# A hybrid HGRN2, mLSTM and expert-choice MoE layer: the mixer loop put in another order, router logits with tokens on partitions, g1 folded into w_out, head norms applied at the store

## The chip, the cores and the metric

The program runs on one core of a Trainium2 chip. The metric is device time in microseconds (us) of one execution, taken as the median of several runs. Beside the times there is one profiled execution, whose trace gives every instruction of the engines: PE (TensorE matmuls; PEld is its weight load), DVE (VectorE), ACT (ScalarE), POOL (GpSimd), and SP, whose queue issues nearly all DMAs here.

## The reference

One layer for 1024 latent tokens of width 1024 and 256 context tokens, all in float32:

```python
u = rms_norm(x, norm1_w) * (1 + sc1) + sh1            # adaLN, sh1..g2 from c @ ada_w + ada_b
p = u @ w_in                                          # HGRN2 q,i,g,f(2 directions); mLSTM q,k (3x3 conv), v, o, gates
hg = hgrn2 forward + hgrn2 backward                   # 4 heads of 128
ml = mlstm forward + mlstm backward                   # 4 heads of 128
hg = hg * rsqrt(mean(hg*hg, head) + eps) * hg_norm_w * silu(p_g)
ml = layer_norm(ml, head) * ml_norm_w * sigmoid(p_o)
x  = x + g1 * (concat(hg, ml) @ w_out)
v  = rms_norm(x, norm2_w) * (1 + sc2) + sh2
aff = softmax(v @ router_w)                           # 16 experts
gate, idx = top_k(aff.T, 128)                         # each expert takes its 128 best tokens
y  = (silu(v[idx] @ w_gate) * (v[idx] @ w_up)) @ w_down * gate
x  = x + g2 * scatter_add(y, idx)
out = rms_norm(x, final_norm_w)
```

## The kernel before, in words

The code states the work in one order; a planner then lays every engine's instructions out as a fixed list. It runs a simulated clock over the program and gives an engine, at each moment, the first instruction in program order that it thinks ready. On the chip each list is then executed strictly in order, whatever the real times are. DMAs issued by SP are such a list too. Tiles are named; a name with `bufs=n` has n slots, and a new tile waits until the oldest one is read for the last time.

Matmuls that must be exact to float32 split each operand in a high and a low part (`wh`/`wl`, `mh`/`ml`) and add three products.

The stages, with their lines:

- Modulation, context work and projections (to 180 us), then the HGRN2 heads, four in turn (lines 649 to 701, to 455 us). At the end of a head, for each half of the tokens, ACT squares the output `po` with a running sum into `hgr` (698), copies it to `ob` (700, one slot named `hgo`), and SP stores it in DRAM as `d_hg` (701). After all heads, DVE and POOL turn `hgr` into 1/rms at once (720, 721).
- The convolution stage (lines 798 to 1099, to about 713 us). `ORD` (1077) is an order written by hand: a number n is `conv(n)` (812) for one group of 128 mLSTM channels; "v..." and "o..." are pieces of the V projection and the output gates (863); "kN" transposes and scales the keys of token block N (`back_k`, 840) and "uN" makes the backward state before that block from them (`back_u`, 845); "M" opens the pools of the mixer and loads the first three row blocks of w_out (`load_wo`, 1073); "S0", "S1" are `scores`, "O0" is `outputs`, "L0" `normed`.
- The mixer loop (1135 to 1179), over eight blocks of 128 tokens. `scores(cc)` (932) loads `qkx` and `MB`, the latter the row maxima broadcast over 128 partitions; makes q.k on PE (939); the decay `E` on ACT and DVE (943 to 945, 949); and `MB` through POOL, ACT and DVE (946, 947, 950). `outputs(cc)` (954) updates the forward state (`ml_u`, 964) and makes the heads (975, 976 on PE, 977 to 981 on ACT and DVE). `normed` (986) layer-norms them (POOL power at 155, ACT 995). `mixed(cc)` (998) multiplies by the gates on DVE (1005 for the HGRN2 heads with `hgr`, 1006 for the mLSTM heads), transposes on PE (1011) and splits into `mh`, `ml` (1012 ACT, 1013 DVE; one slot each). `mixer(cc)` (1016) is the product with w_out (1026: 2 x 24 matmuls), times g1 (1027), plus x (1028), stored as `d_acc` (1029). `router` (1047) norms the row and stores `d_v` (1052 to 1056). `logits` (1032) transposes the row (1038, 1039), multiplies it with the router weights to 16 x 128 (1042) and copies that to SBUF (`lt`, 1044); `affinity` (1062) transposes it back to 128 x 16 on PE (1063) and takes the softmax (1065 to 1069).
- Ahead of the loop w_out's eight row blocks are scaled by the head norm weights and split into `woh`, `wol` (1117 ACT, 1118 DVE) through three slots `wor`.
- In iterations 5 and 6 the loop also sorts affinities for the top-k and makes the first four split expert weights. After it come the rest of the top-k (to 942 us) and the 16 experts (to 1500 us), with 512 KB weight loads running ahead through a list of free buffers (`raw_load`, 883), and the final norm.

The loop's program order in iteration cc is: `scores(cc+2)`, `outputs(cc+1)`, `mixer(cc)`, `router` and `logits` of cc-1, `normed` and `mixed` of cc+1, `affinity(cc-1)`.

## Time and profile before

| | us |
|---|---|
| median of 3 runs | 1559.41 (1558.56 to 1561.38) |
| the profiled execution | 1559.33 |
| its span, first to last instruction | 1557.6 |

| engine | busy, us | share of the span |
|---|---|---|
| PE matmul | 1447.8 | 93% |
| PEld weight load | 1206.9 | 77% |
| DVE | 1230.4 | 79% |
| ACT | 864.7 | 56% |
| POOL | 174.8 | 11% |

Matmuls overlap in the pipeline, so a busy PE row does not mean that PE runs at its peak; and PE's clock has two levels, 1.2 and 2.4 GHz, so a stretch is read by its busy time and by its granted clock together. An average over the program says little here: the stages have different limits, and the change touches the stretch from about 260 to 950 us. Times in the rows are us from the span's start. In a timeline row, what stands in brackets is how long the engine was idle just before it and whose end released it.

### The profile page before, as it was taken

How to read it: one execution, taken by the hardware profiler on the slowest of the kernel's cores; microseconds unless marked ns; L12 is line 12 of the kernel's file. 1: busy time of each engine (PE TensorE's matmuls, PEld its weight loads, DVE VectorE, ACT ScalarE, POOL GpSimd, SP SyncE). 2: the span in 40 equal slices, each digit the busy share in tenths (PEclk: the TensorE clock that was granted, in tenths of full speed). 3: DMA queues.
4: the chain of work that ended last, by engine and by line, in shares of the span. 5: the costliest groups of instructions: out<-in, count | busy, mean ns of one | idle time of the engine just before them, and what ended most of it. 6: DMA issues, size and time to landing. Idle time of an engine off the chain costs nothing.

```text
span 1557.6 us, 23134 instructions
## 1 busy us (share of the span) xinstructions
PE 1447.8 (93%) x8121; PEld 1206.9 (77%) x8121; DVE 1230.4 (79%) x2193; ACT 864.7 (56%) x1454; POOL 174.8 (11%) x136
## 2 busy tenths in 40 slices
PE   7999999999999998988888947999999999999996
PEld 2899878888898896977677735888888888888764
DVE  3685577888866859546757796999999999998887
ACT  3764424334434343345545315777787787777775
POOL 0000000000002221210222110010000000000003
PEclk9999999999999998989898977999999999999998
DMA  9741311220334254276753486999999999999942
GB/s 268 258 128 31 110 54 35 75 82 22 115 102 142 82 149 149 72 194 211 223 183 112 158 320 211 370 391 374 386 387 384 385 389 383 387 376 362 352 141 109
DMA packets 181201, 337.31 MB, mean 217 GB/s; under 512 B 13560, under 2 KB 108348, under 8 KB 181084
## 3 DMA queue, kind: packets, MB, share of 16 engines
q1 hardware_dynamic: 176472, 319.99, 58.0%
q0 software_dynamic: 4320, 15.73, 4.1%
q8 instruction: 64, 1.05, 0.3%
q14 instruction: 53, 0.43, 0.1%
q10 hardware_dynamic: 292, 0.10, 0.0%
HBM read 303.38 MB, written 32.39 MB: 216 GB/s over the span
## 4 chain that ended last, share of the span: by engine, by line
PE 64%; DVE 13%; DMA 10%; issue 6%; ACT 4%; POOL 2%; SPq 0%; ACTq 0%; POOLq 0%; DVEq 0%
PE mm L1303 22%; PE mm L278 11%; PE hg L1303 10%; PE mm L286 5%; PE hg L350 3%; DMA MB<-d_nm 3%; DVE cacc L827 3%; PE hg L215 2%; PE ms L1288 2%; DMA wraw<-in_w_in_dram 1%; PE mm L1026 1%; PE ms L382 1%; POOL cacc L825 1%; DMA wraw<-in_ada_w_dram 1%; PE mm L496 1%
## 5 line engine op out<-in xcount | busy, mean ns | idle before, releaser
L286 PE MATMUL mm<-whi,uh 128*128 128x256 f32 (+1 forms) x512 | 145.6, 284 | 3.0 <-DVE Sb L386 1.3
L286 PE MATMUL mm<-wlo,uh 128*128 128x256 f32 (+1 forms) x512 | 145.1, 283 | 0.0
L286 PE MATMUL mm<-whi,ul 128*128 128x256 f32 (+1 forms) x512 | 144.8, 283 | 0.0
L253 DVE TENSOR_TENSOR wlo<-wraw,whi 128x512 fp32r<-128x512 f32 x96 | 64.7, 686 | 49.5 <-ACT whi L252 49.0
L286 PEld LDWEIGHTS mm<-whi,uh 128*128 128x128 f32 x512 | 96.7, 189 | 5.2 <-DVE Sb L386 1.5
L286 PEld LDWEIGHTS mm<-whi,ul 128*128 128x128 f32 x512 | 96.8, 189 | 0.0
L286 PEld LDWEIGHTS mm<-wlo,uh 128*128 128x128 f32 x512 | 96.3, 188 | 0.3
L1303 PE MATMUL mm<-qkx,xT 128*128 128x512 f32 x256 | 83.7, 408 | 0.6 <-ACT xT L1289 0.3
L827 DVE SCALAR_TENSOR_TENSOR cacc<-pad,cols,cacc 128x1024 f32<-128x1024 f32 x48 | 63.6, 1325 | 24.4 <-POOL cacc L825 23.6
L1303 PE MATMUL mm<-E,xT 128*128 128x512 f32 x256 | 81.2, 398 | 0.4 <-ACT E L922 0.4
L1303 PE MATMUL mm<-MB,xT 128*128 128x512 f32 x256 | 80.8, 397 | 0.0
L252 ACT CAST whi<-wraw 128x512 fp32r<-128x512 f32 x96 | 58.4, 620 | 38.3 <-PE mm L278 24.8
L344 ACT COPY hgc<-hgK 128x512 f32<-128x512 f32 x56 | 35.5, 634 | 78.1 <-DVE hgK L363 38.6
L350 PE MATMUL hg<-hgQ,hgc 128*128 128x128 f32 x448 | 65.9, 291 | 1.0 <-DVE hgQ L366 1.0
L350 PEld LDWEIGHTS hg<-hgQ,hgc 128*128 128x128 f32 x448 | 57.8, 191 | 10.8 <-issue 6.9
L278 PE MATMUL mm<-uh,whi 128*128 128x512 f32 x192 | 63.4, 405 | 0.0
L278 PE MATMUL mm<-ul,whi 128*128 128x512 f32 x192 | 63.4, 404 | 0.0
L278 PE MATMUL mm<-uh,wlo 128*128 128x512 f32 x192 | 61.5, 399 | 0.0
L297 DVE SCALAR_TENSOR_TENSOR ac<-wraw,csil,ac 128x256 f32<-128x256 f32 x112 | 55.9, 499 | 4.1 <-DMA wraw<-in_ada_w_dram 2.2
L1303 PEld LDWEIGHTS mm<-E,xT 128*128 128x128 f32 x256 | 47.9, 189 | 13.7 <-ACT E L922 1.7
L1303 PEld LDWEIGHTS mm<-MB,xT 128*128 128x128 f32 x256 | 48.2, 188 | 11.9
L359 DVE COPY_PREDICATED hgA<-lm,hg 128x512 f32<-128x512 uint8 x56 | 41.4, 740 | 18.4 <-PE hg L350 17.1
(602 smaller groups left out, 4304.2 us busy)
## 6 DMA issues: line engine op xcount, KB each, us to landing
wraw<-in_w_in_dram SPq DMA_DIRECT2D x48, 512.0 KB
wl<-in_exp_w_up_dram SPq DMA_DIRECT2D x34, 512.0 KB
wh<-in_exp_w_up_dram SPq DMA_DIRECT2D x34, 512.0 KB
wh<-in_exp_w_gate_dram SPq DMA_DIRECT2D x34, 512.0 KB
wl<-in_exp_w_gate_dram SPq DMA_DIRECT2D x34, 512.0 KB
wraw<-in_ada_w_dram SPq DMA_DIRECT2D x32, 512.0 KB
wl<-in_exp_w_down_dram SPq DMA_DIRECT2D x29, 512.0 KB
wh<-in_exp_w_down_dram SPq DMA_DIRECT2D x29, 512.0 KB
```

Of the source, the lines that this page charges most:

```text
L215: T.matmul(pm[0:2, :256], csil[:, k, :], adas[i, k // 4][:, k % 4, :, :], start=(k == 0), stop=(k == 7))
L252: S.copy(hi[:, :, cs], src)
L253: V.tensor_sub(lo[:, :, cs], src, hi[:, :, cs])
L278: T.matmul(o, l, r[:, k, i * n:(i + 1) * n], start=(k == 0 and q == 0), stop=(k == 7 and q == 2))
L286: T.matmul(o, l[:, k, ts], r, start=(k == 0 and q == 0), stop=(k == 7 and q == 2))
L297: V.scalar_tensor_tensor(ac, a2[:, k % 4, :], csil[:, k, 0:1], ac, op0=OP.mult, op1=OP.add)
L344: S.copy(view(kc, 0, [[h, 2], [2 * h, 256 // h], [1, h]]), view(K, 0, [[512 + h, 2], [2 * h, 256 // h], [1, h]]))
L350: T.matmul(pb[:, cc, :], kc[:, cc * P:(cc + 1) * P], view(Q, cc * P, pat), start=True, stop=True)
L359: V.copy_predicated(A, lmask[h].unsqueeze(1).to_broadcast([P, 4, P]), scores(h))
L827: V.scalar_tensor_tensor(acc, tap(t), tapw(t, r), acc, op0=OP.mult, op1=OP.add)
L1288: T.transpose(pt[:, k, :], view(src, 4 * q + k, [[8, P]]), ident)
L1303: T.matmul(o, l[:, k, :], r[:, 512 * j:512 * j + 512], start=(k == 0 and p_ == 0), stop=(k == 7 and p_ == 2))
```

## The change

What it does, in the order of the code:

- At the end of a half head, 1/rms is made at once (DVE add of eps, POOL power on 128 x 4) and POOL multiplies `ob` by it ahead of the store. The two instructions after the last head go.
- `mixed` multiplies the HGRN2 heads by their gates in one 128 x 512 instruction, on DVE for cc up to 2 and on POOL from 3, in place of four with `hgr`.
- `mh`, `ml` have two pairs; the second takes two of the three `wor` slots.
- g1 is multiplied into each row block of w_out on POOL (128 x 1024) right after its load; the product with g1 after the mixer's matmuls goes. g1's broadcast is loaded at "M", ahead of the w_out loads.
- `logits` makes 128 x 16 directly (the transposed row as the stationary operand); the copy to `lt` and the transpose in `affinity` go.
- `ORD`: each state update "u" comes a step later after its "k", behind a convolution or another piece; "S1" stands ahead of "O0".
- The loop: `scores(2)` and `normed(outputs(1))` are put ahead of it, and iteration cc is `mixer(cc)`, `scores(cc+3)`, `mixed(cc+1)`, `normed(outputs(cc+2))`, then `router`, `logits`, `affinity` of cc-1.
- One expert weight is loaded in iteration 0 and not three; two `wor` slots and g1's join the free buffers after the loop.

The diff, cut to its core:

```diff
@@ heads' store
                 S.copy(ob, po)
+                r = hgr[:, 4 * hf:4 * hf + 4, h:h + 1]
+                V.tensor_scalar(r, r, EPS, None, op0=OP.add)
+                G.tensor_tensor(r, r, mhalf[:, 0:4].unsqueeze(2), op=OP.pow)
+                G.tensor_mul(ob, ob, r.to_broadcast([P, 4, P]))
                 load(d_hg[4 * hf:4 * hf + 4, :, h * P:(h + 1) * P].rearrange("c p v -> p c v"), ob)
...
-    V.tensor_scalar(hgr, hgr, EPS, None, op0=OP.add)
-    G.tensor_tensor(hgr, hgr, mhalf[:, 0:1].unsqueeze(2).to_broadcast([P, 8, 4]), op=OP.pow)
@@ mixed
-        for h in range(4):
-            V.scalar_tensor_tensor(mix[:, h, :], hg[:, h, :], hgr[:, cc, h:h + 1], go[:, h, :], op0=OP.mult, op1=OP.mult)
+        (G if cc > 2 else V).tensor_mul(mix[:, 0:4, :], hg, go[:, 0:4, :])
...
-        mh, ml_ = tb("mh", [8, P], 1, F32R), tb("ml", [8, P], 1, F32R)
+        mh, ml_ = mixT[cc % 2]
@@ mixer
-            V.tensor_mul(pb, pb, g1b[:, cs])
             V.tensor_add(xm[:, cs], xm[:, cs], pb)
@@ logits
-            T.matmul(pl[0:16, 0:P], rwa[:, k, :], xT[:, k, :], start=(k == 0), stop=(k == 7))
-        lt = tb("lt", [P], 2)
-        S.copy(lt[0:16, :], pl[0:16, 0:P])
-        return pl, lt
+            T.matmul(pl[:, 0:16], xT[:, k, :], rwa[:, k, :], start=(k == 0), stop=(k == 7))
+        return pl
@@ affinity
-        T.transpose(pl[:, P:P + 16], lt[0:16, :], ident[:16, :16])
...
-        V.scalar_tensor_tensor(lg, pl[:, P:P + 16], r2, cb, op0=OP.mult, op1=OP.add)
+        V.scalar_tensor_tensor(lg, pl[:, 0:16], r2, cb, op0=OP.mult, op1=OP.add)
@@ load_wo
         load(wors[k], w_out[k * P:(k + 1) * P, :])
-
-    ORD = (5, 4, "v004", 6, "v044", 7, "v104", 0, "v144", "k7", 1, "u7", "k6", "k5", "u6", "k4", 2, "u5", 3,
-           "o004", "u4", "k3", "o044", "u3", "k2", "u2", "o104", "k1", "M", "u1", "S0", "O0", "L0", "S1", "o144")
+        G.tensor_mul(wors[k], wors[k], g1b)
+
+    ORD = (5, 4, "v004", 6, "v044", 7, "v104", 0, "v144", 1, "k7", "k6", 2, "u7", "k5", "u6", 3, "k4", "u5",
+           "o004", "k3", "u4", "o044", "k2", "u3", "k1", "u2", "o104", "M", "u1", "S0", "S1", "O0", "L0", "o144")
@@ ahead of the loop
+    mixT = [(tb("mh", [8, P], 1, F32R), tb("ml", [8, P], 1, F32R))]
+    mx = {0: mixed(0, sc.pop(0))}
...
+    mixT.append([tl("wor", [1024], 3, F32R).rearrange("p (a b) -> p a b", b=P) for _ in range(2)])
+    free.append([tl("wor", [1024], 3)])
...
+    sc[2] = scores(2)
+    hs = {1: normed(outputs(1, *sc.pop(1)))}
     for cc in range(8):
+        prev_xm, xm = xm, mixer(cc, *mx.pop(cc))
+        if cc < 5:
+            sc[cc + 3] = scores(cc + 3)
+        if cc < 7:
+            mx[cc + 1] = mixed(cc + 1, hs.pop(cc + 1))
         if cc < 6:
-            sc[cc + 2] = scores(cc + 2)
-        if cc < 7:
-            hsum = outputs(cc + 1, *sc.pop(cc + 1))
-        prev_xm, xm = xm, mixer(cc, *mx_)
-        if 0 < cc < 7:
-            rt = router(cc - 1, prev_xm), *logits(prev_xm)
-        if cc < 7:
-            mx_ = mixed(cc + 1, normed(hsum))
-        if 0 < cc < 7:
-            affinity(cc - 1, *rt)
+            hs[cc + 2] = normed(outputs(cc + 2, *sc.pop(cc + 2)))
+        if cc:
+            affinity(cc - 1, router(cc - 1, prev_xm), logits(prev_xm))
```

## Rows read from the trace of the kernel before

**Rows 1.** Stretches between mixer stores: length; busy PE, PEld, DVE, ACT, POOL; clock; DMA; GB/s.
```profile
738.40:763.40 25.00, 20.71 (x119) 16.77 (x117) 18.16 (x47) 11.93 (x32) 6.36 (x4) 0.96 0.77 226
763.40:794.70 31.30, 26.42 (x150) 22.66 (x150) 20.02 (x55) 17.82 (x48) 8.33 (x5) 0.87 0.59 216
794.70:821.40 26.70, 22.19 (x123) 19.07 (x124) 18.44 (x50) 12.63 (x36) 6.02 (x4) 0.90 0.46 138
821.40:848.60 27.20, 25.05 (x141) 21.97 (x141) 17.17 (x50) 12.78 (x35) 6.56 (x4) 0.88 0.38 136
848.60:874.40 25.80, 23.93 (x134) 20.01 (x134) 17.89 (x53) 9.89 (x28) 3.97 (x3) 0.91 0.35 123
874.40:891.70 17.30, 17.02 (x101) 14.36 (x99) 16.27 (x72) 7.33 (x18) 4.00 (x3) 1.00 0.41 139
891.70:910.60 18.90, 14.94 (x63) 11.52 (x63) 18.51 (x84) 3.94 (x10) 2.90 (x2) 0.91 0.68 229
```

**Rows 2.** SP's issues in order of time: the first and last mixer store.
```profile
738.39 0.33 SPq L1029 DMA_DIRECT2D d_acc<-xm  x1
...
910.57 0.33 SPq L1029 DMA_DIRECT2D d_acc<-xm  x1
```

**Rows 3.** Who waited for whom, 738 to 849 us: total us, times, longest.
```profile
ACT E L943 <- DMA MB<-d_nm: 26.3, 5, 7.3
...
PE hg L1063 <- ACT lt L1044: 9.2, 4, 3.5
```

**Rows 4.** ACT in order of time within one block: start, us, line, idle before.
```profile
784.47 1.57 ACT L943 ACTIVATE E<-MB,gT 128x128 f32<-128x128 f32 x5 [7.27 <-DMA MB<-d_nm]
785.95 1.64 ACT L995 ACTIVATE hsum<-hsum,nb,r 128x128 f32<-128x128 f32 x4
...
790.98 1.06 ACT L947 ACTIVATE MB<-MB 128x1024 f32<-128x1024 f32 x1 [0.70 <-POOL MB L946]
791.94 0.24 ACT L1044 COPY lt<-hg 16x128 f32<-16x128 f32 x1
```

**Rows 5.** PE in order of time, same block: the two stops behind the mixer.
```profile
792.24 0.23 PE L1063 MATMUL hg<-ident,lt 16*128 16x16 f32 x1 [1.40 <-ACT lt L1044]
...
795.70 1.09 PE L480 MATMUL ms<-ident,qkx 128*128 128x128 f32 x4 [1.92 <-DVE ml L1013]
```

**Rows 6.** Groups by line, 713 to 912 us: busy, mean ns of one, idle before.
```profile
L1055 POOL TENSOR_TENSOR vt<-vt,B2b 128x1024 f32<-128x1024 f32 x7 | 16.6, 2378 | 14.9 <-DVE vt L1054 10.1 <-DVE den L979 4.8
L1042 PE MATMUL hg<-xT,rwa 128*16 128x128 f32 x112 | 14.0, 274 | 0.8 <-ACT xT L1039 0.8
L1005 DVE SCALAR_TENSOR_TENSOR mix<-kin,hgr,go 128x128 f32<-128x128 f32 x32 | 12.7, 415 | 0.4 <-DMA go<-d_go 0.4
...
L1027 DVE TENSOR_TENSOR mm<-mm,g1b 128x512 f32<-128x512 f32 x16 | 10.9, 690 | 6.1 <-PE mm L1026 6.0
```

**Rows 7.** DVE and POOL in order of time: one DVE product beside POOL.
```profile
855.40 2.46 DVE L1005 SCALAR_TENSOR_TENSOR mix<-kin,hgr,go 128x128 f32<-128x128 f32 x1
...
855.36 2.35 POOL L1055 TENSOR_TENSOR vt<-vt,B2b 128x1024 f32<-128x1024 f32 x1 [4.77 <-DVE den L979]
```

**Rows 8.** ACT and DVE in order of time: the last of eight w_out row blocks.
```profile
732.54 1.14 ACT L1117 ACTIVATE wh<-wor,cols 128x1024 fp32r<-128x1024 f32 x1
...
733.71 1.28 DVE L1118 SCALAR_TENSOR_TENSOR wl<-wor,cols,wh 128x1024 fp32r<-128x1024 f32 x1 [0.79 <-ACT wh L1117]
```

**Rows 9.** A stretch of the convolution stage, and PE's longest stop in it.
```profile
600.00:610.00 10.00, 3.08 (x13) 2.15 (x12) 9.61 (x15) 4.67 (x9) 4.70 (x2) 0.71 0.69 222
...
608.47 0.77 PE L496 MATMUL mm<-v,mkt 128*128 128x129 f32 x2 [5.27 <-DVE mkt L486]
```

**Rows 10.** The heads' store: its waiters (us, times), and POOL's power in `normed`.
```profile
  ACT hgo L698: 8.8, 4
...
863.04 1.02 POOL L155 TENSOR_TENSOR r<-r,mhalf 128x4 f32<-128x4 f32 x1 [5.33 <-DVE mx L1066]
```

**Rows 11.** A stretch of the experts, columns as in Rows 1.
```profile
1000.00:1100.00 100.00, 100.00 (x473) 81.09 (x472) 96.72 (x106) 79.49 (x94) 7.38 (x6) 1.00 1.02 382
```

More of the change, by code (lines that the diff above doesn't have):

```diff
@@ L1060, in router, with affinity @@
         return r2
-    def affinity(cc, r2, pl, lt):
-        T.transpose(pl[:, P:P + 16], lt[0:16, :], ident[:16, :16])
+    def affinity(cc, r2, pl):
         lg, mx, sm_ = aff[:, cc // 4, cc % 4, 0:16], tb("mx", [1]), tb("sm", [1])
-        V.scalar_tensor_tensor(lg, pl[:, P:P + 16], r2, cb, op0=OP.mult, op1=OP.add)
+        V.scalar_tensor_tensor(lg, pl[:, 0:16], r2, cb, op0=OP.mult, op1=OP.add)
         V.tensor_reduce(mx, lg, axis=AX.X, op=OP.min)
@@ L1085, in tile_hybrid_block @@
             tl = tile_in(mpa)
+            g1b = bcast(tl("g1b", [1024]), d_g[0])
             for k in range(3):
@@ L1106, in tile_hybrid_block @@
     tb = tile_in(mpb)
-    def first():
-        if isinstance(sc[0], tuple):
-            sc[0] = outputs(0, *sc[0])
-        if "L0" not in ORD:
-            sc[0] = normed(sc[0])
-        return mixed(0, sc.pop(0))
-    mx_ = first()
+    mixT = [(tb("mh", [8, P], 1, F32R), tb("ml", [8, P], 1, F32R))]
+    mx = {0: mixed(0, sc.pop(0))}
     for k in range(8):
@@ L1124, in tile_hybrid_block @@
     load(mods, d_g[1:3].rearrange("g (p k) -> p g k", k=8))
-    g1b = bcast(tb("g1b", [1024]), d_g[0])
     xm, rt = None, None
-    free.extend([tl("wor", [1024], 3)] for _ in range(3))
+    mixT.append([tl("wor", [1024], 3, F32R).rearrange("p (a b) -> p a b", b=P) for _ in range(2)])
+    free.append([tl("wor", [1024], 3)])
     def old(n):
@@ L1134, in tile_hybrid_block @@
     tmp = [[tops[:, i] for i in (0, 1, 6)], [tops[:, i] for i in (2, 3, 7)], [tops[:, i] for i in (4, 5, 6)]]
+    sc[2] = scores(2)
+    hs = {1: normed(outputs(1, *sc.pop(1)))}
     for cc in range(8):
-        if cc < 6:
-            sc[cc + 2] = scores(cc + 2)
-        if cc < 7:
-            hsum = outputs(cc + 1, *sc.pop(cc + 1))
-        prev_xm, xm = xm, mixer(cc, *mx_)
-        if 0 < cc < 7:
-            rt = router(cc - 1, prev_xm), *logits(prev_xm)
-        if cc < 7:
-            mx_ = mixed(cc + 1, normed(hsum))
-        if 0 < cc < 7:
-            affinity(cc - 1, *rt)
-        if cc == 6:
-            r6 = router(6, xm)
+        prev_xm, xm = xm, mixer(cc, *mx.pop(cc))
[3 more added lines that the diff above has]
+            mx[cc + 1] = mixed(cc + 1, hs.pop(cc + 1))
+        if cc < 6:
+            hs[cc + 2] = normed(outputs(cc + 2, *sc.pop(cc + 2)))
+        if cc:
+            affinity(cc - 1, router(cc - 1, prev_xm), logits(prev_xm))
         if cc == 0:
@@ L1157, in tile_hybrid_block @@
             V.tensor_reduce(cb, view(pb, 0, [[1, 16], [16, 8]]), axis=AX.X, op=OP.add)
-            raw_load(3)
+            raw_load(1)
         if cc in (1, 3, 5):
@@ L1186, in tile_hybrid_block @@
     raw_load(18)
-    p6, p7 = logits(prev_xm), logits(xm)
-    r7 = router(7, xm)
-    free.extend([tb(n, [1024], m)] for n, m in (("g1b", 1), ("A2b", 1), ("B2b", 1), ("xm", 2)))
+    affinity(7, router(7, xm), logits(xm))
+    free.extend([tb(n, [1024], m)] for n, m in (("A2b", 1), ("B2b", 1), ("xm", 2)))
+    free.extend([tl("wor", [1024], 3)] for _ in range(2))
+    free.append([tl("g1b", [1024])])
     raw_load(4)
-    affinity(6, r6, *p6)
-    affinity(7, r7, *p7)
     if stop in ("ml", "mid"):
```

## The prediction, made before the changed kernel was run

> **What bounds the kernel now.** I read the busy slices of the page first. From about 950 us the experts keep PE full at full clock, with DVE and the DMAs nearly as full [rows 11]; the change leaves that work alone, so it moves by as much as its start moves. The heads and most of the convolution stage are also full of matmuls. What is left is the mixer loop, and I cut it at its stores: eight of them, the first at 738.4 us, the last at 910.6 [rows 2], so seven intervals of 172.2 us together. The windows between them [rows 1] are to be read by length, busy PE and clock. The five with a whole block's work take 25 to 31 us; PE is idle for 25.0 - 20.7 = 4.3, then 4.9, 4.5, 2.2 and 1.9 us, and runs at a granted clock of 0.87 to 0.96. The last two take 17.3 and 18.9 us, with DVE busy for 16.3 and 18.5 of them: they belong to DVE, which sorts there.
>
> With two clock levels, a mean of 0.87 means that a quarter of the time was at 1.2 GHz, and busy time times (1 - clock) is what full clock would have saved: 0.8 + 3.4 + 2.2 + 3.0 + 2.2 + 0 + 1.3 = 12.9 us over the seven. The idle time sums to 172.2 - 150.3 = 21.9 us. So a loop in which PE never stopped would take 172.2 - 21.9 - 12.9 = 137.4 us, and 34.8 us is all that this loop can give back.
>
> Why PE stops is in the list of waits and in one block of the timelines. ACT waits 26.3 us in five pieces for the broadcast load `MB` [rows 3]. In the block shown it stands still for 7.27 us until 784.5, then makes `E`, and only then the layer norm of the heads (785.95) and, behind the exponential of `MB` (790.98), the copy of the logits to `lt` (791.94) [rows 4]. Both had been waiting in ACT's fixed list. PE's own list has the 16 x 16 transpose of the logits next: it stops there for 1.40 us in this block [rows 5] and for 9.2 us in four blocks [rows 3]. Behind it, PE stops for 1.92 us for a bank that `ml`'s subtraction frees [rows 5]; `ml` is late because the norm was late. The `MB` load itself is not needed until a block later. The stop comes from what is queued behind it.
>
> **The change, part by part.** *Logits.* The copy (0.24 us on ACT [rows 4]) and the transpose (0.23 us on PE [rows 5]) go, and with them the 9.2 us of stops [rows 3]. The product has as many matmuls with 16 columns in place of 128 to stream [rows 6]; its weight loads grow from 16 to 128 columns, so I cost it as unchanged. What is late next is `mh`, `ml`, which the change also moves ahead.
>
> *Order of the loop and two operand pairs.* Between two mixers PE still has logits, transposes, scores and outputs, so PE's work doesn't fall. But `normed(cc+1)` now stands before `mixer(cc)`, so nothing of `mixed(cc+1)` waits for ACT behind the new `MB`; the second pair lets its split be written while the mixer reads the first. `MB` has two slots as before, its load still starts when `outputs` of two blocks earlier ends, and ACT can still stop for it. Behind such a stop are then the copies of `mh` and of the logits' row; PE has outputs and logits to do before it needs the first. I take the five full intervals: of 17.8 us idle, the 9.2 us, and a third of the other 8.6, 3; of 11.6 us of lost clock, 60%, 7, because the clock fell in the stretches with stops. That is -19 (bounds: -5, half of the transpose's stops, to -29, all).
>
> *DVE relief.* The product with g1 goes: 16 x 0.69 = 10.9 us [rows 6]. The four gate products go from DVE for cc from 3 on: 4 x 0.34 us of a block. In the last two intervals that is 2 x (1.4 + 1.4) = 5.5 us of DVE's 34.8 [rows 1]; PE has 0.3 + 4.0 idle and 1.3 of clock there, 5.6. I take -4 (0 to -5.5). After the last mixer one g1 product, the copy and the transpose are on the chain itself: 0.69 + 0.24 + 0.23, and DVE finishes the merges of the first six blocks earlier: -2 together (-1 to -4).
>
> *What goes to POOL.* Five gate products of 128 x 512: no row shows one; a 128 x 1024 sum on POOL takes 2.38 us [rows 6], so by half of its length 1.2 us each. POOL has 4 to 8 us of work in an interval [rows 1], so they fit. But the rows show a price: a DVE product that takes 0.3 to 0.4 us took 2.46 us when it started beside a POOL sum, and ended with it [rows 7]. Only in the blocks with cc above 2 can this happen, up to 5 x 1.2 = 6 us of DVE time; outside the last two intervals DVE has 7 to 11 us spare [rows 1], so I leave it in the bounds above.
>
> The Trainium skill says the same more sharply ("SBUF — State Buffer", "Who interferes with whom"): the port pair that GpSimd shares with VectorE is an exclusive lock, and a DVE instruction with two SBUF inputs waits out a GpSimd instruction that reads SBUF. The pair of rows agrees. It speaks against this change, which adds POOL products in three stages; by that rule the rival priced below as "POOL in the way" would come true.
>
> *g1 into w_out.* Eight POOL products of 2.4 us. Three can run long before they are needed, once g1 and the rows have landed. The other five pass through three slots, each now load, POOL, ACT, DVE, with 2.4 us more. The last block of rows is at present ready on ACT at 733.7 and on DVE at 735.0 [rows 8], while the first mixer is under way (stored at 738.4). The last row block comes two turns of the ring after the first ones: 2 x 2.4 = 4.8 us later at least, 5 x 2.4 = 12 at most if POOL takes them one behind the other and holds DVE off. Outputs and scores of the next blocks can fill part of it. I take +3 (0 to +12). g1's load of 512 KB at "M" is in front of the w_out rows and of the first `MB` in SP's queue; I leave that in these bounds.
>
> *Heads' store.* Each of eight half heads puts an add, a power (1.0 us [rows 10]) and a 1.2 us product between the copy and the store, and `hgo` has one slot: ACT waits for that store now 8.8 us in four times [rows 10], and would wait some 2.5 to 3 us longer each time, with casts of the next weights queued behind. The weights have several slots ahead of PE, which hides it: +1 (0 to +6).
>
> *Order of the convolution stage.* PE's longest stop there is a state update that waits 5.27 us for keys that DVE scales late; in that stretch of 10 us PE is busy for 3.1 at 0.71 clock [rows 9]. With a convolution or a piece between "k" and "u" PE's list has a full product there. Idle 6.9 us and some clock behind it are to be had; a stop of the same kind can appear elsewhere. I take -6 (+2 to -12).
>
> *Expert weights.* Two fewer 512 KB loads run ahead. Demand in the experts is met now with PE full [rows 11]. I cost it at nothing; were the loads to run dry at the end, 1 MB at 382 GB/s is +2.7.
>
> **The sum.** -19 - 4 - 2 + 3 + 1 - 6 = -27, on the profiled execution's own 1559.33 us, which lies within 0.1 us of the median of the runs: 1532.
>
> **The rivals.** *PE dense.* The stops vanish entirely: the loop gives all 34.8, the convolution stage 10, the rest as above: 1559 - 34.8 - 10 - 2 + 3 = 1515. For it: nearly all stops in the rows hang on one queue, and the change takes out what hung there. Against it: DVE's load in the last two intervals, and `MB` still loads no earlier.
>
> *The stop moves.* The fixed lists put the `mh` copies behind the next `MB` again, and PE waits at the first matmul of the mixer in place of the transpose. Then only half of the transpose's stops is won, -5 in the full intervals, -2 in the last two, -2, -4 in the convolutions, +3, +1: 1550. For it: ACT's 26.3 us of waiting have not been removed, and a simulated clock that placed `lt` badly may place `mh` badly. Against it: `mh` has outputs and logits of PE time as slack, `lt` had none.
>
> *POOL in the way*, the slower side. The five late w_out products and DVE's low parts take turns on the port, and the first mixer waits for the last: +12; the eight stores add +6 to the heads; the loop gains only 5 + 2 because DVE waits for POOL in each block, the convolution stage nothing: 1559 + 18 - 9 = 1568. It decides when the last row block is ready later than 735.0 us by more than the loop and the convolution stage win, that is by over 10 us. For it [rows 7]; against it, POOL's low load, and that mixer 0 can take its rows one by one.
>
> *Nothing changes.* The planner orders by readiness, so moving lines may leave the lists as they are, and the gains and the POOL prices cancel: 1559. Against it: the transpose and the g1 product are gone whatever the order.
>
> **How the numbers follow.** Forecast (own range 1522 to 1543) 0.55; PE dense 0.15; the stop moves 0.18; POOL in the way 0.08; nothing changes 0.04. From 1514 to 1553 holds the first three but for their far ends. 0.2%, some 3 us, is about what a measurement of this kernel tells from no change. Faster: 0.55 + 0.15 + 0.17 = 0.87; slower: 0.08; within: 0.05.
>
> **What would show it.** Right: no PE stop between logits and outputs; the five full intervals at 21 to 24 us in place of 25 to 31, with a clock above 0.95; no stop over 3 us at a state update; the last low part of w_out within 5 us of the first mixer's need. Wrong: ACT's wait for `MB` followed by PE waiting for `mh` or `ml`; DVE products of over 2 us beside POOL in each block; the first store of the loop later than 738.4 us by more than the convolution stage won. If the loop shrinks by 20 us and the total doesn't, I would look at the stretch between the last store and the first expert matmul.

## The result, and the profile after

| | before | after |
|---|---|---|
| median, measured side by side, us | 1558.99 (1557.13 to 1561.38) | 1572.47 (1569.05 to 1574.98) |
| the profiled execution, us | 1559.33 | 1569.05 |
| its span, us | 1557.6 | 1566.9 |

The ratio of the times is 1.0084, 95% interval 1.0060 to 1.0108: the changed kernel is slower by 9 to 17 us, where 27 us less was forecast. The stretch behind the mixer loop did not change: from the last store to the end it is 1557.6 - 910.57 = 647.0 us before and 1566.9 - 919.05 = 647.9 after, and the experts still run full. So 8.5 of the 9.3 us between the two traces lie ahead of that store. The execution profiled after the change is the fastest of its four, which is why the traces hold less than the 13.5 us between the medians.

The line numbers of the changed kernel differ a little: its mixer matmuls are on L1027, the sum with x on L1028, the transposes of the mixed heads on L1012, `E` on L945, w_out's high and low parts on L1110 and L1111, the g1 product on L1073. First the loop, cut at its stores as in [rows 1], with the same columns:

```profile
749.80:774.10 24.30, 19.20 (x115) 16.19 (x113) 16.58 (x43) 11.16 (x32) 7.59 (x5) 1.00 0.79 260
774.10:798.50 24.40, 21.64 (x124) 18.94 (x124) 14.17 (x43) 10.53 (x29) 6.37 (x4) 0.92 0.51 174
798.50:826.20 27.70, 23.49 (x134) 20.67 (x134) 15.69 (x44) 12.59 (x35) 8.51 (x5) 0.89 0.41 133
826.20:852.70 26.50, 22.70 (x135) 20.31 (x135) 15.37 (x44) 13.30 (x36) 9.12 (x6) 0.94 0.41 140
852.70:875.70 23.00, 19.71 (x105) 17.14 (x106) 14.55 (x41) 8.04 (x22) 3.93 (x3) 0.93 0.40 137
875.70:901.50 25.80, 23.25 (x115) 19.90 (x115) 18.38 (x66) 9.57 (x25) 5.23 (x4) 0.80 0.41 133
901.50:919.10 17.60, 17.13 (x97) 14.22 (x98) 16.14 (x86) 4.26 (x10) 2.93 (x2) 1.00 0.74 257
```

The five full intervals shrank from 136 to 125.9 us, where 117 was forecast; the last two grew from 36.2 to 43.4. The loop takes 169.2 us in place of 172.2. PE's stops have not become less: it is idle in the five intervals for 19.2 us, before for 17.7. They are shorter because they hold 54 matmuls fewer, while the last two hold 48 more, and because the lower clock (busy time times one less the clock) cost 7.0 us in place of 11.6. And the loop starts late, which the first and last store show, against 738.39 and 910.57 in [rows 2]:

```profile
749.81 0.32 SPq L1029 DMA_DIRECT2D d_acc<-xm  x1
...
919.05 0.33 SPq L1029 DMA_DIRECT2D d_acc<-xm  x1
```

The first store is 11.4 us later; the first mixer matmul was only 1.4 us later (722.9 against 721.5). The first mixer itself took longer. In order of time on POOL, ACT and DVE, the first g1 product after a long idle time, and the last row block of w_out, which was ready at 733.7 and 735.0 in [rows 8]:

```profile
723.33 2.37 POOL L1073 TENSOR_TENSOR wor<-wor,g1b 128x1024 f32<-128x1024 f32 x1 [10.12 <-DMA wor<-in_w_out_dram]
...
740.02 2.37 POOL L1073 TENSOR_TENSOR wor<-wor,g1b 128x1024 f32<-128x1024 f32 x1
...
743.23 1.14 ACT L1110 ACTIVATE wh<-wor,cols 128x1024 fp32r<-128x1024 f32 x1
...
744.39 1.29 DVE L1111 SCALAR_TENSOR_TENSOR wl<-wor,cols,wh 128x1024 fp32r<-128x1024 f32 x1
```

The list of waits from 721 to 920 us (total us, times, longest), to be read against [rows 3]:

```profile
PE ms L1012 <- ACT mkt L484: 8.6, 2, 4.7
PE mm L1027 <- DVE wl L1111: 6.1, 3, 2.3
PE mm L977 <- DVE xm L1028: 4.8, 2, 3.3
...
ACT E L945 <- DMA MB<-d_nm: 14.2, 5, 4.6
```

PE's stop at the logits' transpose is gone, and in its place PE waits at the transposes of the mixed heads for a bank that ACT's scaling of the keys frees, and at the outputs for one that DVE's sum with x frees. ACT still stands still for `MB`, 14.2 us in place of 26.3.

The convolution stage did what was asked of it and lost it again. The ten microseconds of [rows 9] are full now (first fence), but the list of waits from 560 to 725 us has two new ones behind it (second):

```profile
600.00:610.00 10.00, 10.00 (x49) 8.23 (x48) 3.79 (x11) 5.80 (x9) 4.80 (x2) 1.00 0.84 264
```

```profile
PE mm L496 <- ACT mkt L484: 8.9, 1, 8.9
PE mm L278 <- DVE Sb L386: 4.4, 1, 4.4
```

### The profile page after: what moved, and what is told of

It reads as the page before. It is cut to its first block, busy times and chain, and to the rows that moved or that the text cites. A ratio compares the mean times of both kernels' runs of the same rounds, so it can differ in the third digit from the quotient of the medians.

```text
span 1566.9 us, 23090 instructions
## 1 busy us (share of the span) xinstructions
PE 1445.8 (92%) x8113; PEld 1209.0 (77%) x8113; DVE 1229.3 (78%) x2155; ACT 864.3 (55%) x1446; POOL 215.9 (14%) x164
## 4 chain that ended last, share of the span: by engine, by line
PE 70%; DVE 12%; DMA 7%; ACT 4%; issue 4%; POOL 2%; ACTq 0%; SPq 0%; POOLq 0%; DVEq 0%
PE mm L1293 21%; PE mm L278 12%; PE hg L1293 11%; PE mm L286 9%; PE hg L350 4%; DMA MB<-d_nm 3%; PE hg L215 2%; PE ms L1278 2%; PE mm L1027 1%; PE ms L382 1%; DVE cacc L829 1%; DVE ac L297 1%; DMA wraw<-in_ada_w_dram 1%; POOL MB L948 1%; PE hg L1383 1%
## 5 line engine op out<-in xcount | busy, mean ns | idle before, releaser
L829 DVE SCALAR_TENSOR_TENSOR cacc<-pad,cols,cacc 128x1024 f32<-128x1024 f32 x48 | 67.4, 1404 | 17.9 <-POOL cacc L827 17.3
L1308 POOL DMA_INDIRECT vt<-d_v,idx x16 | 16.3, 1016 | 332.9 <-PE ms L1278 252.3
```

What stands on the lines that cost most here:

```text
L829: V.scalar_tensor_tensor(acc, tap(t), tapw(t, r), acc, op0=OP.mult, op1=OP.add)
L1308: G.indirect_dma_start(out=xg, out_offset=None, in_=d_v, in_offset=bass.IndirectOffsetOnAxis(ap=idx[:, e:e + 1], axis=0))
```

## The experiments

Each was measured against the kernel before on the same chip. A price in us below is the ratio less one, times 1557.

| run | what it is | median, us | ratio to before, 95% |
|---|---|---|---|
| e1_order_only | before, conv order | 1556.45 | 0.9991 (0.9977 to 1.0005) |
| e2_heads_only | before, heads' rms at the store | 1561.63 | 1.0022 (1.0010 to 1.0034) |
| e3_g1_only | before, g1 in w_out on POOL | 1569.57 | 1.0074 (1.0051 to 1.0098) |
| e4_loop_only | before, loop order, pairs, logits | 1558.47 | 1.0001 (0.9983 to 1.0018) |
| e5_g1_dve | as e3, product on DVE | 1566.01 | 1.0056 (1.0036 to 1.0076) |
| e6_heads_q | as e2, slot of `hgo` freed early | 1563.17 | 1.0039 (1.0026 to 1.0052) |
| e7_logits_only | before, logits | 1557.95 | 1.0001 (0.9988 to 1.0014) |
| e8_loop_mb3 | as e4, third `MB` slot (blocks 2, 5) | 1539.51 | 0.9892 (0.9865 to 0.9918) |
| e10_loop_mb3b | as e4, third `MB` slot (blocks 3, 6) | 1538.63 | 0.9887 (0.9867 to 0.9908) |
| e11_after_mb3 | after, third `MB` slot | 1563.35 | 1.0046 (1.0028 to 1.0065) |
| e12_heads_poolq | as e2, store from POOL's queue | 1565.58 | 1.0058 (1.0040 to 1.0076) |
| e13_before_mb3 | before, third `MB` slot | 1541.72 | 0.9905 (0.9889 to 0.9922) |
| e14_loop_mb3b_g1 | as e10, g1 in w_out on POOL | 1545.19 | 0.9914 (0.9894 to 0.9934) |
| e15_loop_mb3_order | as e8, conv order | 1539.19 | 0.9888 (0.9871 to 0.9904) |
| e16_after_mb3_vt | as e11, router's sum on DVE | 1548.39 | 0.9935 (0.9919 to 0.9952) |
| e17_after_mb3_mix | as e11, gate product on DVE | 1550.84 | 0.9961 (0.9949 to 0.9973) |
| e18_heads_q_poolq | e6 and e12 together | 1557.75 | 1.0009 (0.9999 to 1.0019) |

### The parts, one at a time

The edit of each is the change's own diff, cut to one part. My theory was that each part fails in its own place; the rivals put the loss on one of them, or on scatter.

**Conv order** (only `ORD`).

```diff
-    ORD = (5, 4, "v004", 6, "v044", 7, "v104", 0, "v144", "k7", 1, "u7", "k6", "k5", "u6", "k4", 2, "u5", 3,
+    ORD = (5, 4, "v004", 6, "v044", 7, "v104", 0, "v144", 1, "k7", "k6", 2, "u7", "k5", "u6", 3, "k4", "u5",
...
```

> The kernel before with the new conv and backward order (ORD) alone. The prediction's step says -6 us (about 1553). Theory A, from the trace of the changed kernel: the conv matmuls end 7 us earlier against the start of conv, but 4 us of it come back as a state-update wait (8.9 us once) before the o-gates' end, so -3 us (1556). Rival B, that the gain is given back entirely by the first mixer: 1559, with the first store of the mixer loop still 258.7 us after the first conv matmul.

-1.4 us, not told from nothing. From the first to the last convolution matmul it takes 481.4 to 632.2 = 150.8 us, where before takes 479.7 to 635.3 = 155.6; the last o-gate matmul comes 228.4 us after the first convolution matmul, before 228.9. So 4.8 us are won and 4.3 given back in between, to stops that the list of waits (560 to 725 us) names:

```profile
PE hg L939 <- DVE gsg L306: 11.6, 1, 11.6
PE mm L278 <- DVE Sb L386: 4.6, 1, 4.6
```

**Heads' rms at the store** (the four added lines, and one gate product for four, on POOL from block 3 on as in the change).

```diff
+                r = hgr[:, 4 * hf:4 * hf + 4, h:h + 1]
+                V.tensor_scalar(r, r, EPS, None, op0=OP.add)
+                G.tensor_tensor(r, r, mhalf[:, 0:4].unsqueeze(2), op=OP.pow)
+                G.tensor_mul(ob, ob, r.to_broadcast([P, 4, P]))
...
```

> The kernel before with the heads' rms applied at their store alone (the mixer reads it with one product in place of four). The prediction's step says +1 us (1560). Theory A: the product on POOL is put ahead of the next head's sum qk on POOL's list, so the HGRN transposes' wait for that sum goes from 2.9 to about 6.4 us and the first conv matmul comes 3 to 4 us later: 1562.5. Rival B: the 3.5 us by which conv starts later in the changed kernel are the scatter between launches, and the time stays at 1559.

+3.4 us. The loop has no part in it: from the first to the last store it takes 911.58 - 742.00 = 169.6 us, before 172.2. What makes the price is below.

**g1 into w_out** (one line in `load_wo`, the product after the mixer gone).

```diff
+        G.tensor_mul(wors[k], wors[k], g1b)
...
-            V.tensor_mul(pb, pb, g1b[:, cs])
```

> The kernel before with g1 folded into w_out's rows on POOL alone (no product after the mixer). The prediction's sum says +3 ahead of the first mixer and about -4 in the last two loop intervals: 1558. Theory A: POOL's eight products go through the ring of three row buffers and put the last w_out pair 10 us later, so the first mixer store comes about 10 us later; the loop itself gains at most 3: 1566. Rival B: the delay of the first mixer is given back since scores and outputs of the next blocks run in it: 1559, with the first store 10 us later and the last one where it was.

+11.5 us, the largest price, and almost the whole of the loss. The first store is at 748.86, 10.5 us later; the last at 921.50, so the loop takes 172.6 us as before, though 10.9 us of DVE work [rows 6] are gone from it. The relief of DVE was worth nothing. In order of time, ACT's first three row blocks in the kernel before (first fence), then in e3 the same, POOL's fourth, fifth and last product, and DVE's last low part:

```profile
714.90 3.22 ACT L1117 ACTIVATE wh<-wor,cols 128x1024 fp32r<-128x1024 f32 x3
```

```profile
719.76 3.21 ACT L1118 ACTIVATE wh<-wor,cols 128x1024 fp32r<-128x1024 f32 x3
...
725.78 5.18 POOL L1075 TENSOR_TENSOR wor<-wor,g1b 128x1024 f32<-128x1024 f32 x2 [13.19 <-DMA wor<-in_w_out_dram]
...
740.98 2.39 POOL L1075 TENSOR_TENSOR wor<-wor,g1b 128x1024 f32<-128x1024 f32 x1
...
745.38 1.28 DVE L1119 SCALAR_TENSOR_TENSOR wl<-wor,cols,wh 128x1024 fp32r<-128x1024 f32 x1 [0.59 <-ACT wh L1118]
```

POOL was idle for 13.2 us before the fourth row block: the rows arrive late, one for each slot that is given back, so the five late products can't be done ahead. From ACT's first row block to the end of DVE's last low part it takes 26.9 us, before 20.1. That is the longer way through the ring, 6.8 us; the other 4.9 us of delay are there before ACT starts on the first block, and what makes them was not followed up.

**The loop part** (order, pairs and logits; one 512 KB expert load in iteration 0 in place of three and g1's broadcast loaded at "M", as in the change).

```diff
+        prev_xm, xm = xm, mixer(cc, *mx.pop(cc))
+        if cc < 5:
+            sc[cc + 3] = scores(cc + 3)
+        if cc < 7:
+            mx[cc + 1] = mixed(cc + 1, hs.pop(cc + 1))
         if cc < 6:
-            sc[cc + 2] = scores(cc + 2)
+            hs[cc + 2] = normed(outputs(cc + 2, *sc.pop(cc + 2)))
...
```

> The kernel before with the loop's part alone: one block further ahead, two operand pairs, logits with tokens on partitions; g1 stays a product after the mixer, the heads' rms and the conv order stay as before. The prediction's steps say -21 us (1538). Theory A: the stop moves from the logits' transpose to the mixed transposes that wait for ACT's mkt scaling in the bank ms, so the loop gains about 3 to 5 us only: 1555. Rival C: the loop gained little in the changed kernel only because the g1 products and the conv order shifted what precedes it; alone it gives 1540 to 1545.

+0.2 us. The part that was to give 21 gives nothing. The five full intervals are shorter here too, 126.5 us, with PE idle for 18.9; but the last two take 39.5, and the first store comes 7.0 us later (745.41), since ACT stands still for 3.9 us for a load of `MB` ahead of w_out's last two row blocks. One block in order of time on SP, ACT, POOL, DVE and PE shows why:

```profile
753.10 0.37 SPq L936 DMA_DIRECT2D MB<-d_nm  x1
...
757.40 0.16 DVE L993 SCALAR_TENSOR_TENSOR nb<-mv,r 128x4 f32<-128x4 f32 x1
...
763.60 0.70 ACT L943 ACTIVATE E<-MB,gT 128x128 f32<-128x128 f32 x2 [9.43 <-DMA MB<-d_nm]
764.20 1.63 ACT L995 ACTIVATE hsum<-hsum,nb,r 128x128 f32<-128x128 f32 x4
...
767.66 2.43 POOL L946 TENSOR_TENSOR MB<-MB,mu_b 128x1024 f32<-128x1024 f32 x1 [7.70 <-ACT E L943]
768.26 2.38 DVE L1006 SCALAR_TENSOR_TENSOR mix<-go,hsum 128x512 f32<-128x512 f32 x1
...
770.70 1.12 PE L1011 MATMUL ms<-ident,mix 128*128 128x128 f32 x4 [5.97 <-DVE mix L1006]
```

`MB` is asked for at 753.10 and lands 10.5 us later. Two of `E`'s instructions stand ahead of the heads' layer norm (L995) on ACT's list, though the norm's inputs are ready at 757.6. So norm, gate product and transposes wait, just as the copy of the logits had waited before: the same cause with another victim. The gate product then takes 2.38 us beside POOL's sum, and PE stops for 5.97.

**Logits alone.**

```diff
-            T.matmul(pl[0:16, 0:P], rwa[:, k, :], xT[:, k, :], start=(k == 0), stop=(k == 7))
+            T.matmul(pl[:, 0:16], xT[:, k, :], rwa[:, k, :], start=(k == 0), stop=(k == 7))
...
-        T.transpose(pl[:, P:P + 16], lt[0:16, :], ident[:16, :16])
```

> The kernel before with the logits made with tokens on partitions, nothing else. The prediction put the 9.2 us of PE's stops at the transpose down to this edit, plus 0.5 us on the last chain: 1550. Theory A: the stop moves to the next matmul that waits for the norm behind ACT's wait for MB (the transposes of the mixed heads), so only 0 to 2 us come: 1556. Either way no PE stop is left between the logits and the outputs.

+0.2 us, as theory A has it, but the stop is not where it put it: no transpose is left to stop at, and PE stops at the logits' own matmuls, while ACT waits for `MB` as long as ever (721 to 912 us):

```profile
PE hg L1042 <- ACT xT L1039: 12.6, 5, 6.8
...
ACT E L943 <- DMA MB<-d_nm: 30.3, 5, 7.3
```

The parts add up, as far as their intervals tell (some 5 us either way together): -1.4 + 3.4 + 11.5 + 0.2 = +13.7 us, against +13.1 of the whole change.

### The load behind the stops

If ACT's wait for `MB` is the cause, then a third slot, which lets the load start a block earlier, must give what the reordering didn't.

```diff
-        qk, MB = tl("qkx", [8, P], 2), tl("MB", [8, P], 2)
+        qk, MB = tl("qkx", [8, P], 2), MBx[0] if cc in (2, 5) else tl("MB", [8, P], 2)
...
-    free.append([tl("wor", [1024], 3)])
+    MBx.append(tl("wor", [1024], 3).rearrange("p (a b) -> p a b", b=P))
```

> The loop part alone as in e4_loop_only, with a third slot for the broadcast MB: blocks 2 and 5 take the w_out row buffer that went to the expert weights (which get it four blocks later). Theory A: nearly all that is left of the loop's stops hangs on ACT standing still for MB (23.9 us in four waits in e4), so with loads a block earlier the waits fall below 6 us, the five full intervals to 21 to 23 us each, and the time to 1542 to 1547. Rival B: the stop moves once more, to the banks that ACT's scaling of the keys and DVE's sum with x free: 1554 to 1558. Rival C: the load is late because the DMA engines are full and not because of its slot; then MB lands as late as before and the time stays at 1558.

-16.8 us: theory A, a little below its range. The windows between stores:

```profile
741.80:767.10 25.30, 20.73 (x100) 17.96 (x99) 22.41 (x51) 12.66 (x32) 7.71 (x5) 0.82 0.66 219
767.10:787.30 20.20, 20.04 (x126) 17.58 (x127) 18.13 (x51) 11.10 (x32) 6.26 (x4) 1.00 0.74 210
787.30:807.70 20.40, 20.40 (x131) 18.00 (x131) 17.77 (x50) 11.78 (x34) 6.26 (x4) 1.00 0.70 178
807.70:828.30 20.60, 20.60 (x135) 18.41 (x134) 18.24 (x51) 13.16 (x36) 6.27 (x4) 1.00 0.52 178
828.30:848.60 20.30, 20.29 (x130) 17.75 (x128) 17.00 (x48) 8.63 (x23) 6.00 (x3) 1.00 0.48 161
```

Four blocks run at 20.2 to 20.6 us, full PE and full clock: there PE bounds the loop. What is left is the first interval. Block 2's `MB` takes the buffer that w_out's last rows give up late; ACT stands still for it and PE behind it:

```profile
733.20 2.44 ACT L943 ACTIVATE E<-wor,gT 128x128 f32<-128x128 f32 x8 [6.04 <-DMA wor<-d_nm]
...
738.73 1.11 PE L1011 MATMUL ms<-ident,mix 128*128 128x128 f32 x4 [8.46 <-DVE mix L1006]
```

So the next run gave the third slot to blocks 3 and 6:

```diff
-        qk, MB = tl("qkx", [8, P], 2), MBx[0] if cc in (2, 5) else tl("MB", [8, P], 2)
+        qk, MB = tl("qkx", [8, P], 2), MBx[0] if cc in (3, 6) else tl("MB", [8, P], 2)
```

> As e8_loop_mb3, but blocks 3 and 6 take the third slot and not 2 and 5, so that block 2's MB needn't wait until w_out's last row block is done with that buffer. Theory A: the load for block 2 starts some 8 us earlier, ACT's wait of 6.0 us for it goes, and with it most of PE's 8.5 and 4.6 us of stops around the first store: 1530 to 1534. Rival B: the load stands behind w_out's rows on the DMA engines and lands as late: 1539 as e8.

0.9887, not told from e8: rival B in its effect. PE's 8.5 us go, and PE waits 7.0 us for the load of `qkx` in the next interval instead, 29.3 us long; in that stretch the core's DMA engines move 253 GB/s at a busy share of 0.77.

What are order and pairs worth beside it? The same slot went into the kernel before. A first run (e9, 1542.4 us) gave the buffer to the expert weights in iteration 4, before block 6 had read its `MB`; the run that stands gives it one iteration later.

> The kernel before with a third slot for MB alone (blocks 3 and 6 take one w_out row buffer, which goes to the expert weights only in iteration 5). Theory A: the slot does most of it: 1540 to 1545, and order, pairs and logits are worth the 3 to 5 us between this and e8 or e10. Rival B: the loop order is needed as well: 1550 or more.

-14.8 us, theory A. The slot alone is most of it; order, pairs and logits together are worth 2 to 3 us more, which the intervals don't tell from nothing. That the load now comes earlier is in SP's issues: the last of the eight loads of `MB`, in the kernel before and in e13.

```profile
829.34 0.39 SPq L936 DMA_DIRECT2D MB<-d_nm  x1
```

```profile
795.58 0.37 SPq L936 DMA_DIRECT2D MB<-d_nm  x1
```

ACT's wait for these loads falls from 26.3 to 11.3 us. In e13 PE still stops 7.6 us at the logits' transpose. With the slot an expert weight is loaded later, too: iteration 0 loads two in e13 and none in e8 and e10. That fewer loads make the gain is ruled out by e4, which loads one in place of three and gained nothing.

The conv order (`ORD` of the change) on top of e8:

> As e8_loop_mb3, with the changed kernel's conv order. Theory A: as in e1, the 7 us won in the convolutions come back as state-update waits: 1537 to 1540. Rival B: the mixer's first block is no longer the bound behind them and the order pays: 1533 to 1536.

0.9888: theory A, the conv order adds nothing. e8, e10 and e15 beat both kernels by some 17 us and more, and can't be told from each other.

### What the g1 fold costs

```diff
-        G.tensor_mul(wors[k], wors[k], g1b)
+        V.tensor_mul(wors[k], wors[k], g1b)
```

> The kernel before with g1 folded into w_out's rows as in e3_g1_only, but the eight products on DVE in place of POOL. Theory A: the 12.5 us of e3 come from the ring of three row buffers, whose every turn got a longer chain (load, product, ACT, DVE, next load); a DVE product takes about 1.2 us where POOL's took 2.4 to 2.7, so half of the price stays: 1563 to 1565. Rival B: the price is POOL's, by its length and by holding up DVE; then it goes nearly whole and the time is 1557 to 1559. Rival C: DVE is the bound there (it was busy for some 25 of 27 us in the changed kernel's first mixer) and the price is as before or more: 1569.

+8.7 us in place of 11.5, nearest to theory A and above its numbers. The first store is at 744.97 (POOL: 748.86). From ACT's first row block to the last low part it takes 24.4 us, so the way through the ring is 4.3 us longer than before, with POOL's product 6.8. By these two, most of the price stays whichever engine takes the product, and POOL's length and its hold on DVE are the smaller part; the intervals of e3 and e5 overlap, so the share is rough. Nor is rival C excluded: DVE was busy for 17.6 of the 20.7 us from the first mixer matmul to the first store.

The fold on POOL, as in e3, on top of e10:

> As e10_loop_mb3b, with g1 folded into w_out on POOL. Theory A: the fold costs what it cost alone, the first store 6 to 10 us later and nothing in the loop: 1549 to 1551. Rival B: the fold alone makes the 25 us between e11 and e10, since with the product gone from DVE's list POOL's sums fall beside DVE's work on the heads: 1560 or more, with a clock below 0.9 in most intervals. Rival C: with MB's stops gone DVE is what bounds the first intervals, and its 11 us of g1 products saved pay for the late start: 1540.

1545.2, between theories A and C: +4.2 us against e10, where e3 was +11.5 against before. The first store is 10.4 us later (749.69 against 739.25), but the loop is 2.3 us shorter, and the load of `qkx` costs 3.9 in place of 7.0. The two traces differ by 8.2 us, more than the ratios say, so how much of the late start is won back is only roughly known; that a late first mixer lets the crowded loads catch up is a guess. One rival falls here: e10 loads g1's broadcast ahead of w_out's rows as well, without the fold, and its first store is on time. So the load itself is not what the fold costs.

### Why the changed kernel gained so little from the slot

The third slot goes into the changed kernel as in e10.

> The changed kernel with the third slot of MB (blocks 3 and 6), all else as changed, g1 folded on POOL and the heads' rms at the store included. Theory A: the parts add up, so it stays above e10 by the price of the two folds, 12 + 4 us, less the conv order's 1: about 1548. Rival B: with the stops gone the loop is bound by DVE in its last intervals and by PE elsewhere, so the g1 product's 11 us of DVE time that are saved pay now: 1540 or less.

Both theories fell: 1563, by the ratios 21 us above e14, which has the same loop and the same fold. Its full intervals take 22 to 28 us again with nearly no wait for `MB` (5.6 us). One of them in order of time on POOL, DVE and PE, and then its stretches (columns as in [rows 1]):

```profile
801.45 2.36 POOL L1053 TENSOR_TENSOR vt<-vt,B2b 128x1024 f32<-128x1024 f32 x1 [1.16 <-DVE vt L1052]
801.89 2.08 DVE L980 TENSOR_TENSOR den<-den,emn 128x2 f32<-128x2 f32 x3
...
804.89 0.50 PE L1027 MATMUL mm<-wh,wor 128*128 128x512 f32 x1 [1.99 <-DVE hsum L983]
```

```profile
796.00:804.80 8.80, 6.90 (x62) 6.63 (x59) 8.26 (x18) 4.37 (x14) 4.19 (x3) 1.00 0.47 158
804.80:815.40 10.60, 10.43 (x33) 8.50 (x33) 5.96 (x22) 4.92 (x17) 2.89 (x2) 0.52 0.83 168
```

Three DVE steps on 128 x 2 numbers take 2.08 us until POOL's sum is over. The heads are late by that, PE stops for 1.99 us on their bank, and then does its next 10.43 us of work at a granted clock of 0.52, the lower level. By (1 - 0.52) x 10.43 that costs another 5.0.

```diff
-        G.tensor_add(vt, vt, B2b)
+        V.tensor_add(vt, vt, B2b)
```

> As e11_after_mb3, with the router's sum with B2b (128 x 1024) on DVE in place of POOL. Theory A: in e11 that POOL sum of 2.4 us holds up a small DVE step of the heads' norm (2.08 us in place of 0.2), PE stops for 2 us on the bank behind it and then runs at half clock for 10; with the sum on DVE (1.3 us) the stop goes and the full intervals fall from 25 to 28 us to 20 to 23: 1548 to 1552. Rival B: the stop is one of the fixed lists' order, and DVE's longer list only moves it: 1560 to 1565.

-17.3 us against e11, the time of theory A (the two traces differ by 11.8). The five full intervals are 24.5, 25.2, 21.8, 23.2 and 21.1 us, in place of 26.0, 24.7, 27.9, 24.7 and 22.2. DVE's step is free, as theory A has it: shortest, median and longest of its 20 in the five intervals, in ns, in e11, e16 and (below) e17.

```profile
L980 DVE TENSOR_TENSOR den<-den,emn x20: 133/152/2216, 754.6 to 858.1; 128x2 f32<-128x2 f32 x20
L980 DVE TENSOR_TENSOR den<-den,emn x20: 142/150/164, 757.6 to 850.2; 128x2 f32<-128x2 f32 x20
L980 DVE TENSOR_TENSOR den<-den,emn x20: 141/154/2033, 757.2 to 850.6; 128x2 f32<-128x2 f32 x20
```

In the block shown, PE's stop falls from 1.99 to 0.92 us and the clock of the interval rises from 0.82 to 1.00. But the stop as such does not go: over the five intervals PE waits for `hsum` 6.9 us in place of 4.8. What falls is the time at the lower clock: busy time times one less the clock gives 6.0 us in place of 13.5.

```diff
-        (G if cc > 2 else V).tensor_mul(mix[:, 0:4, :], hg, go[:, 0:4, :])
+        V.tensor_mul(mix[:, 0:4, :], hg, go[:, 0:4, :])
```

> As e11_after_mb3, but the gate product of the HGRN2 heads on DVE in every block (in e11 on POOL from block 3 on); POOL keeps the router's sum. Theory A: it is the two POOL sums and products together that reach DVE's step of the norm, so with one fewer the full intervals fall to 20 to 23 us and the time to 1548 to 1552, as in e16. Rival B: the router's sum alone does it, also with the product on DVE: 1560 to 1564.

-13.2 us against e11, again in theory A's range, though one interval of 26.0 is left. But here DVE's step is held up as in e11 (2.03 us at the longest), and the time at the lower clock falls all the same, to 5.9 us. So taking either of two POOL instructions out of a block is worth 13 to 17 us, and that POOL's sum holds up DVE's small step is shown by e16; that this hold-up makes the 21 us is not shown. Every such edit also gives the planner another list, and which stops then bring the clock down stays open.

### The heads' store

From the first output matmul of the first head to the first convolution matmul it takes 220.5 us in the kernel before and 224.1 in e2. There ACT waits for the store to give back `hgo`, 4.2 us once where it was 2.3, 11.5 us in all where it was 8.8, and DVE's new add stands behind that. The first cure was the slot; `od` is the half's `hgQ`, which nothing reads any more, and it is stored in place of `ob`:

```diff
-                G.tensor_mul(ob, ob, r.to_broadcast([P, 4, P]))
+                od = Qs[hf][:, 0, :].rearrange("p (c v) -> p c v", c=4)
+                G.tensor_mul(od, ob, r.to_broadcast([P, 4, P]))
```

> The kernel before with the heads' rms at the store as in e2_heads_only, but POOL's product writes into the head's dead query tile hgQ, which is stored, so that the one slot of hgo is free as soon as the product has read it, and not when the store has landed. Theory A: the 4.5 us of e2 come from ACT waiting for that slot, with DVE's new add, DVE's keys and POOL's sum qk late behind it; so they go: 1557 to 1558. Rival B: they come from the new instructions' places on DVE's and POOL's lists themselves: 1561 to 1562 as in e2.

+6.1 us, no gain, and the stretch takes 227.1. ACT's 11.5 us of waiting for the store are gone, but it waits 9.1 us for POOL's product in their place. And on SP's list a load of modulation weights stands behind the store of the first half head; it lands late, and DVE's sums over it stand ahead of the next product of q (L667), on which POOL's sum and PE wait. SP and DVE in order of time:

```profile
338.41 0.37 SPq L706 DMA_DIRECT2D d_hg<-hgQ  x1
338.88 0.45 SPq L293 DMA_DIRECT2D wraw<-in_ada_w_dram  x1
...
343.05 2.05 DVE L297 SCALAR_TENSOR_TENSOR ac<-wraw,csil,ac 128x256 f32<-128x256 f32 x4 [2.90 <-DMA wraw<-in_ada_w_dram]
345.01 1.28 DVE L667 TENSOR_TENSOR hgqk<-hgqk,mm 128x512 f32<-128x512 f32 x2
```

So the store was taken off SP's list, with `hgo` held as in e2:

```diff
-                load(d_hg[4 * hf:4 * hf + 4, :, h * P:(h + 1) * P].rearrange("c p v -> p c v"), ob)
+                G.dma_start(d_hg[4 * hf:4 * hf + 4, :, h * P:(h + 1) * P].rearrange("c p v -> p c v"), ob)
```

> The kernel before with the heads' rms at the store as in e2_heads_only, but the store is issued from POOL's queue behind its product, not from SP's. Theory C, formed on the traces of e2 and e6: SP's list is in order, so the loads of the modulation weights that follow the store on it wait for POOL's product; DVE's sums over those weights, which stand ahead of the next head's product of q on DVE's list, are late by 3 us, and with them POOL's sum qk and the first transposed products of the head. So the price falls to 0 to 1.5: 1557.5 to 1559. Rival A: hgo's one slot alone makes the price (it is still held until the store has landed): 1561 to 1563.

+9.0 us, and the stretch takes 225.4: theory C fell as the only cause. ACT now waits 5.1 us where it was 4.2, and 15.8 us in all, for a store that POOL issues. With both cures:

> The heads' rms at the store as in e2, with both cures: POOL's product writes into hgQ (the slot of hgo is free early, as in e6) and the store is issued from POOL's queue (SP's list doesn't wait, as in e12). Theory A: the slot and SP's list are two paths of about the same length to DVE's product of q, so only both cures together take the price away: 1557 to 1559. Rival B: the price is in DVE's and POOL's own extra instructions: 1561 to 1565.

+1.4 us (-0.2 to +3.0), inside theory A's numbers: both together take the price down to where it can't be told from nothing. Two paths of one length explain why one cure alone gains nothing; why each alone costs more than none (6.1 and 9.0 us against 3.4) they don't, and that stays open. In the stretch itself 223.0 - 220.5 = 2.5 us are left, and what these are made of was not followed up.

## Why the prediction was wrong, step by step

Of the 40 us between the forecast of -27 and the result, 21 are the loop and the logits (-19 - 2, measured 0.2), some 12 the fold of g1 with the relief of DVE (3 - 4, measured 11.5), 5 the conv order and 2 the heads' store.

**What bounds the kernel.** Right as far as it went: the stops hang on ACT's wait for `MB`, and with a third slot the loop of e8 takes 146.4 us in place of 172.2, four of its blocks 20.2 to 20.6. The step that failed is the sentence "nothing of `mixed(cc+1)` waits for ACT behind the new `MB`". It read the program order as ACT's order. The planner lays lists by its own clock, and it put `E` ahead of the norm again (e4), presumably because `MB` lands earlier on that clock; the run shows the order and not the reason. The text had noted that `MB`'s load starts no earlier and counted it harmless. I had even written that the load "is not needed until a block later" and concluded that what is queued behind it had to be moved; e13 shows that moving the load is worth 14.8 us, and e4 that moving what is queued behind it is worth nothing.

**The loop's -19** is 0.2 in e4, and -3 in the changed kernel. The rival "The stop moves" describes it, down to PE waiting at the mixed heads behind `MB`, and took half of the transpose's stops as won; none were (PE idle for 18.9 us in e4's five full intervals, before 17.7).

**DVE's -4** is 0: with g1 off DVE alone (e3) the loop has the same length, and the last two intervals of the changed kernel are 7.2 us longer. That they "belong to DVE" was misread for the first of them: its row shows PE busy for 17.02 of 17.30 us, longer than DVE.

**Logits and the last chain, -2**: 0.2 in e7, and the stretch behind the last store is 647.9 us in place of 647.0.

**g1 into w_out, +3** is 11.5, at the upper bound of 12. The step's own working put the last row block at least 4.8 us late, then took 3 because other work could fill the gap. It was not filled: in the changed kernel the first mixer starts 1.4 us late and its store comes 11.4 us late, with 6.1 us of PE's waits for low parts in between. And the bounds hold only the ring, which makes 6.8 us in e3; the 4.9 us ahead of ACT's first row block are in none of its terms, so that 12 was a bound is in part luck.

**Heads' store, +1** is 3.4, inside its bounds, and in part for a reason that the step left out: it counted the slot of `hgo`, but not what stands behind the store on SP's list; only with both cured is the price gone (e18).

**Conv order, -6** is -1.4. The stop went as said, and "a stop of the same kind can appear elsewhere" came true.

**Expert weights, 0**: right; the stretch behind the last store stayed within 1 us.

**The rivals.** "POOL in the way" gave 1568 with a chance of 0.08, and came nearest, also in its terms: +12 for the first mixer (11.5), +6 for the heads (3.4), 5 + 2 of the loop (3), nothing from the convolutions (1.4). Its chance was set low because POOL is hardly busy. That was the wrong measure: a row block's path through a ring of three slots and a single POOL sum beside a DVE step count by their length, whatever POOL's share. Still its number is partly luck. The rule quoted with it, from the Trainium skill ("SBUF — State Buffer", "Who interferes with whom"), agrees with e11 and e16: a DVE sum of two 128 x 2 tiles takes up to 2.22 us with the POOL sum there and 0.16 without it. For the g1 fold, by e5, the lock and POOL's length together are only some 2.8 of the 11.5 us.

## What to carry to other kernels

When engines run fixed lists, a late load stalls whatever the planner put behind its first reader; here moving the victim made another one, and only an earlier load (one more buffer, -14.8 us by itself) ended most of it. Before a step is put into a ring of few buffers, add its length to each turn and ask what the last turn's consumer can do meanwhile. A store that now waits for one more engine holds its buffer and also every transfer behind it on its queue: count both.

## What was not expected of the hardware

A PE stop of 1.99 us was followed by 10.43 us of work at a granted clock of 0.52 (e11), so by estimate the stop cost about 7 us. A 512 KB broadcast load took 10.5 us from issue to use while the DMA engines moved some 210 GB/s (e4). And three DVE steps on 128 x 2 numbers took 2.08 us beside a POOL sum of 2.36 us: the smallest steps are held up about as long as a larger one (2.46 us for 128 x 128 in [rows 7]).
